# The lead-in of the first layer reordered: every modulation product and square sum on VectorE, low halves on GpSimd, low-half products last in a block

## The chip, the cores and the metric

The kernel runs on one core of one Trainium2 chip. The metric is the device time of one execution in microseconds (us), as the median of several runs. The engines are named as the profile names them: PE (TensorE; PEld is its weight load), DVE (VectorE), ACT (ScalarE), POOL (GpSimd) and SP (SyncE, which issues all transfers here). Each engine runs its own instructions in the order in which they stand; semaphores hold an instruction until its inputs are there.

## The reference

The reference is a decoder trunk of two layers with a final RMSNorm, for one sequence of 1024 positions and 1024 channels, in float32. Only the first steps of a layer matter here:

```
c_act = silu(c)                                        # once
mod = c_act @ w_ada + b_ada                            # (1, 3072): shift, scale, gate
h = rms_norm(x, norm_g) * (1.0 + scale) + shift
proj = h @ w_in
```

`proj` then feeds a causal pooling mixer, a retention mixer and an RWKV-7 mixer; their gated outputs are projected, merged, projected once more, scaled with `gate` and added to `x`. Everything of that is the same in both kernels, instruction for instruction.

## The kernel before, in words

Activations are held transposed: eight channel tiles `kt` (0 to 7) of 128 channels by 1024 positions, cut in two halves `h` (0 and 1) of 512 positions. One tile is therefore 128x512 float32, 256 KB. A float32 product is made of three faster ones: each operand is split in a rounded high part (`hhi`, `wh`, or a piece of `wbig`) and the rest (`hlo`, `wl`, or another piece of `wbig`), and PE adds high x high, low x high and high x low into one PSUM tile (`acc`), each a product of 128x128 weights with 128x512 columns.

The change touches only the **lead-in**: what comes before the first three output tiles of layer 0 (called lora, k and r, tiles 0, 1 and 2) are complete for both halves, in `acc6`. It is written out by hand under a manual schedule: for PE, DVE, ACT and POOL the order of the code is the order of the instructions. SP is not in that schedule and is ordered by the framework around it. From the end of the lead-in on, an estimated clock and lanes of tasks set the order.

The steps of the lead-in, by the names in the code:

- `xdma`, `wdma`, `aload` issue transfers on SP: the 16 tiles of `x`, the raw weights `wr` of the three output tiles (two pieces each), and 26 tiles of `w_ada` (groups 0 to 5) into a ring of eight slots (`ringG`) and six spare weight buffers (`wada`).
- `sq2(h, j)` squares two tiles on ACT and adds them on DVE (L1142), and PE sums the result over channels by four products with a column of ones (`ssps`), added up over four pairs.
- `rstd(h)` makes the reciprocal root (`rn`) on ACT and DVE, and `rstd_bc` has PE spread it over all partitions in PSUM (`rbc`); `rstd_copy` copies that to SBUF (`rbs`) for POOL.
- `normed(h, kt)` scales a tile of `x` by it, on DVE (L1176, from `rbc`) or POOL (L1174, from `rbs`).
- The modulation comes in six groups: groups 0 to 3 give shift and scale of one channel tile each (kt 0 to 3), group 4 of kt 4 and 5, group 5 of kt 6 and 7. Groups 0 and 1 are done by `ada_pe`: PE multiplies the pieces of `w_ada` as weights with a column of `cact` (16 products of 128x1 a group, `adaps<-cact,ringG`). Groups 2 to 5 are done by `ada`: DVE multiplies and adds in eight steps (L224, L226), the running sum in PSUM (`ada_ps`), the last into SBUF (`ada_acc`), and PE sums that over partitions with products of one column (`adaps<-fixed,ada_acc`). In both, `ada_end` makes `mod` (L258) and `acoef` (L264) on DVE.
- `affine(h, kt)` applies shift and scale on ACT, twice: once rounded into `hhi` (L1182), once in place (L1183). `low` subtracts them into `hlo` (L1188), on DVE or POOL.
- `wsp(j, tile)` splits a raw weight piece: a cast on ACT (L543), a subtraction on POOL (L544).
- `mms(h, kt)` issues a block: nine products, for each of the three output tiles high x high, low x high and high x low of the weights. `acc6[0]` takes half 0 and `acc6[1]` half 1.

Eight channel tiles times two halves give 16 blocks, 144 products. After them `evac` takes the six sums, and PE goes on with 48 products of the next output tile, v.

Of the kernel before, what the change touches and what calls it, by code (L numbers as in the profile page):

```python
# [96 lines left out]
def trunk_kernel(ctx, tc, xT, cvec, pos, vecs, consts, w_ada, w_all, pool_w, lora_w, out):  # L97
# [101 lines left out]
    cth = cp.tile([P, 8], F32, name="cth")  # L199
    nc.scalar.activation(cth, cact, AF.Tanh, scale=0.5)  # L200
    nc.vector.tensor_scalar(cth, cth, 0.5, 0.5, op0=ALU.mult, op1=ALU.add)
    nc.vector.tensor_tensor(cact, cact, cth, op=ALU.mult)
    nc.scalar.activation(fixed[:, 3:4], ones, AF.Sqrt)
# [7 lines left out]
    def ada(l, g, slot_, gap=2200, acc_=t_lt, ws=None):  # L211
# [23 lines left out]
        ada_end(l, g, ps)  # L235
        yield

    def ada_pe(l, g, ws):
        n = len(ADA[g][1])
        W_ = n * P  # L240
        ps = mx("adaps")
        for kt in range(NKT):
            i, o = divmod(kt * W_, HF)
            for m in range(n):
                mmul(
                    ps[:, m : m + 1], ws[i][:, o + m * P : o + (m + 1) * P], cact[:, kt : kt + 1],
                    start=(kt == 0 and m == 0), stop=(kt == NKT - 1 and m == n - 1), skip_group_check=True,
                )
            yield
# [885 lines left out]

    ssp = [None, None]

    def sq2(h, j):
# [2 lines left out]
        nc.scalar.square(b, xin[h][2 * j + 1])
        nc.vector.tensor_tensor(a, a, b, op=ALU.add)  # L1142
# [27 lines left out]
    def normed(h, *kts, pool=False):  # L1170
        for kt in kts:
            x = xin[h][kt]
            if pool:
                nc.gpsimd.tensor_tensor(x, x, rbs[h], op=ALU.mult)  # L1174
            else:
                nc.vector.tensor_tensor(x, x, rbc[h], op=ALU.mult)  # L1176
# [457 lines left out]
```

## Time and profile before

| What | Value |
| --- | --- |
| Runs | 2524.38, 2519.01, 2524.66 us; median 2524.38 |
| Profiled execution | 2522.42 us, span 2520.6 us |
| PE / DVE / ACT / POOL busy, whole span | 96% / 53% / 31% / 32% |
| Mean granted PE clock | 0.982 |
| First product of the lead-in's blocks | at 43.56 us of the span |
| The six `acoef` (shift and scale ready), starts | 37.11, 43.94, 53.93, 60.16, 67.92, 82.09 us |
| First `la` product (after the lead-in and the 48 products of v) | at 105.56 us |

The profile shows one execution. "Span" runs from the first to the last instruction; the execution's own time is 1.8 us longer. A row of the timeline reads: start, length, engine, line, operation, output<-inputs, how many, and in brackets how long the engine sat idle before it and what released it. The length of a matmul is longer than its distance to the next, since matmuls are pipelined. Rows of a grouped view read: line, engine, operation, output<-inputs, shapes, count, then busy time and the mean nanoseconds of one. Each matmul of the sums over partitions, of the modulation and of `rbc` has two records in the trace, so 32 products of the code are 64 there.

### The profile page before, as it was taken

The page shows a single profiled execution, that of the slowest core. Times are in us where ns is not written, and L with a number is a line of the kernel's source. Part 1 is how long each engine was busy: PE and PEld are TensorE (multiplying, and loading weights), DVE is VectorE, ACT ScalarE, POOL GpSimd, SP SyncE. Part 2 cuts the span into 40 slices and gives each one's busy share as a digit, 9 for nine tenths or more (in the row PEclk, how much of TensorE's full clock was granted, in tenths as well). Part 3 has the DMA queues.
Part 4 walks back from the last instruction along what each step waited for, and adds up shares of the span by engine and source line. Part 5 has one row for each costly group of instructions (what it writes and reads, how often), then busy time and mean ns, then how long its engine had stood idle before and what let it go on. Part 6 is the DMA issues. An engine that isn't in the chain of part 4 may idle for free. (4 is left out here: it accounts for less than half of the span.)

```text
span 2520.6 us, 35022 instructions
## 1 busy us (share of the span) xinstructions
PE 2425.8 (96%) x13416; PEld 2007.9 (80%) x13416; DVE 1345.5 (53%) x2548; ACT 792.1 (31%) x1465; POOL 815.7 (32%) x715
## 2 busy tenths in 40 slices
PE   7999999999999999999999999999999999999998
PEld 6778878877787787887878787788878778787888
DVE  4575467368367543467455646835745653412354
ACT  4542242332233223113444224223323312221243
POOL 2321233233133234454442232322313323236441
PEclk9999999999899999999999999999999989999999
DMA  5232112111113224676431211211211121354352
GB/s 203 80 102 72 34 43 85 34 38 60 55 54 100 83 66 134 197 224 196 146 114 50 68 38 34 77 35 43 85 43 38 60 76 51 121 156 126 105 150 76
DMA packets 124216, 223.68 MB, mean 89 GB/s; under 512 B 14096, under 2 KB 17424, under 8 KB 124048
## 3 DMA queue, kind: packets, MB, share of 16 engines
q1 hardware_dynamic: 124048, 221.44, 28.1%
q8 instruction: 105, 1.72, 0.3%
q14 instruction: 63, 0.52, 0.1%
HBM read 174.46 MB, written 46.92 MB: 88 GB/s over the span
## 5 line engine op out<-in xcount | busy, mean ns | idle before, releaser
L544 POOL TENSOR_TENSOR wl<-wr,wh 128x512 fp32r<-128x512 f32 x342 | 454.9, 1330 | 1192.8 <-ACT wh L543 1109.2
L425 PE MATMUL acc<-hhi,wh 128*128 128x512 f32 x2000 | 809.4, 405 | 16.8 <-DVE k L1011 11.0
L425 PE MATMUL acc<-hhi,wl 128*128 128x512 f32 x2000 | 810.7, 405 | 1.7 <-POOL r L1005 1.7
L425 PE MATMUL acc<-hlo,wh 128*128 128x512 f32 x2000 | 811.7, 406 | 0.0
L425 PEld LDWEIGHTS acc<-hhi,wh 128*128 128x128 f32 x2000 | 382.0, 191 | 89.7 <-DVE k L1011 12.6
L425 PEld LDWEIGHTS acc<-hhi,wl 128*128 128x128 f32 x2000 | 382.3, 191 | 71.5 <-issue 2.2
L425 PEld LDWEIGHTS acc<-hlo,wh 128*128 128x128 f32 x2000 | 382.1, 191 | 68.7 <-issue 0.7
L543 ACT CAST wh<-wr 128x512 fp32r<-128x512 f32 x342 | 211.8, 619 | 679.6 <-PE acc L425 457.5
L425 PE MATMUL acc<-olo,wh 128*128 128x512 f32 x384 | 152.9, 399 | 3.9 <-POOL olo L544 3.9
L425 PE MATMUL acc<-oG,wh 128*128 128x512 f32 x384 | 152.4, 398 | 2.2 <-ACT oG L543 1.0
L425 PE MATMUL acc<-oG,wl 128*128 128x512 f32 x384 | 151.6, 395 | 0.0
L956 DVE TENSOR_TENSOR xst<-cy,MT 64x128 f32<-64x128 f32 x128 | 36.2, 283 | 192.3 <-PE cy L425 191.8
L967 DVE SCALAR_TENSOR_TENSOR S<-ch,pc,SP 64x64 f32<-64x64 f32 x256 | 72.4, 283 | 95.0 <-PE ch L425 86.1
L889 DVE TENSOR_TENSOR tm<-MT 64x30 f32<-64x30 f32 (+14 forms) x240 | 103.4, 431 | 7.4
L953 ACT ACTIVATE SP<-S,pc 128x128 f32<-128x128 f32 x128 | 51.4, 401 | 174.0 <-DVE S L967 169.5
L895 DVE TENSOR_TENSOR MT<-MT,tm 64x30 f32<-64x30 f32 (+14 forms) x240 | 99.8, 416 | 7.5
L962 DVE COPY Z<-ch 64x128 f32<-64x128 f32 x128 | 36.1, 282 | 118.1 <-PE ch L425 117.6
L425 PEld LDWEIGHTS acc<-olo,wh 128*128 128x128 f32 x384 | 72.7, 189 | 21.6 <-POOL olo L544 5.8
L425 PEld LDWEIGHTS acc<-oG,wh 128*128 128x128 f32 x384 | 72.7, 189 | 21.1 <-ACT oG L543 2.1
L1459 DVE SCALAR_TENSOR_TENSOR gs<-gs,acc 128x512 f32<-128x512 f32 x64 | 43.4, 682 | 82.1 <-PE acc L425 70.9
L425 PEld LDWEIGHTS acc<-oG,wl 128*128 128x128 f32 x384 | 72.8, 190 | 16.6
L425 PEld LDWEIGHTS ch<-xst,G 128*128 128x128 f32 x512 | 76.7, 191 | 11.6 <-DVE xst L956 0.5
(276 smaller groups left out, 3690.4 us busy)
## 6 DMA issues: line engine op xcount, KB each, us to landing
wr<-in_w_all SPq DMA_DIRECT2D x364, 256.0 KB, 2.7
gd<-gsg SPq DMA_DIRECT2D x80, 256.0 KB, 2.0
gs<-gd SPq DMA_DIRECT2D x80, 256.0 KB, 2.9
wada<-in_w_ada SPq DMA_DIRECT2D x70, 256.0 KB, 3.1
ol<-od SPq DMA_DIRECT2D x64, 256.0 KB, 3.0
ringG<-in_w_ada SPq DMA_DIRECT2D x26, 256.0 KB, 4.3
x<-in_xT SPq DMA_DIRECT2D x16, 256.0 KB, 4.9
od<-po SPq DMA_DIRECT2D x16, 256.0 KB, 2.0
```

Of the source, the lines that this page charges most:

```text
L425: nc.tensor.matmul(out, lhsT=lhsT, rhs=rhs, start=start, stop=stop, **kw)
L543: nc.scalar.copy(hi, src)
L544: eng.tensor_tensor(lo, src, hi.bitcast(F32), op=ALU.subtract)
L889: nc.vector.tensor_tensor(pr, M3[:, i + 1 :, i : i + 1].to_broadcast([64, n, i]), M3[:, i : i + 1, 0:i].to_broadcast([64, n, i]), op=ALU.mult,
L895: nc.vector.tensor_tensor(M3[:, i + 1 :, 0:i], M3[:, i + 1 :, 0:i], pr, op=ALU.add)
L953: nc.scalar.activation(SP, S, AF.Copy, scale=pcc)
L956: nc.vector.tensor_tensor(xst[0:64, :], cy[0:64, 0:P], AV[:, c * P : (c + 1) * P], op=ALU.add)
L962: nc.vector.tensor_copy(Z[0:64, c, :], ch[0:64, 0:P])
L967: nc.vector.scalar_tensor_tensor(Sn[rw, rw], ch[rw, P + 64 * hd : P + 64 * hd + 64], pc[rw, c : c + 1], SP[rw, rw], op0=ALU.mult, op1=ALU.add,
L1459: nc.vector.scalar_tensor_tensor(s, s, 1.0, ps, op0=ALU.add, op1=ALU.mult)
```

## The change: what it does

- **Modulation.** `ada_pe` is gone; all six groups run through `ada`, eight DVE steps each. Group 0's steps stand on DVE right after the square sums; group 1's are mixed with the scaling of half 1 and two low halves.
- **Square sums.** `sq` squares one tile on ACT, and DVE adds the eight squares of a half one after the other; PE then sums once (`sums`), four products a half instead of 16.
- **Scaling.** Of the 16 tiles POOL scales eight (kt 2 to 7 of half 0, kt 4 and 5 of half 1) instead of four. DVE scales the other eight, two of them (kt 6 and 7 of half 1) from the SBUF copy `rbs`; so `rstd_copy` now runs for both halves.
- **Low halves.** POOL makes those of kt 1 to 5 (`both`), DVE those of kt 0, 6 and 7.
- **Blocks.** In `mms` the two products with `hhi` come first for each output tile, and those with `hlo` last. In the blocks of half 1 the third output tile comes after the next group's sum over partitions (`steps(gs[g], 1)`).
- **Transfers.** The raw weights of tile 2 are issued ahead of group 1's `w_ada`, not behind them. `cond_act`, which makes `cact`, moves into the manual schedule, and the table for the root is loaded once, ahead of the squares; before, three tables were loaded on ACT ahead of the first root, now two.

The lines of the diff that the prediction speaks of:

```diff
-        a, b = mo("sq"), t_lt("sq")
-        nc.scalar.square(a, xin[h][2 * j])
-        nc.scalar.square(b, xin[h][2 * j + 1])
-        nc.vector.tensor_tensor(a, a, b, op=ALU.add)
...
+    def sq(h, *kts):
+        for kt in kts:
+            t = t_lt("sq") if kt == 0 else mo("sq")
+            nc.scalar.square(t, xin[h][kt])
+            if kt == 0:
+                ssum[h] = t
+            else:
+                nc.vector.tensor_tensor(ssum[h], ssum[h], t, op=ALU.add)
...
-                mm1(acc6[h][i], wparts[i][kt // 4], kt % 4, h_cur[h][kt], kt == 0, kt == 7)
+    def mms(h, kt, *tiles):
+        r = h_cur[h][kt]
+        for b, js in ((0, (0, 1)), (1, (0,))):
+            for i in tiles or range(3):
+                for j in js:
+                    w = wparts[i][kt // 4][j][:, kt % 4 * P : kt % 4 * P + P]
+                    mmul(acc6[h][i], w, r[b], start=kt == 0 and b == 0 and j == 0, stop=kt == 7 and b == 1)
...
-        gs = [(ada_pe if g < 2 else ada)(0, g, ws=aw[g], **({} if g < 2 else dict(slot_=None))) for g in range(6)]
+        gs = [ada(0, g, None, ws=aw[g]) for g in range(6)]
...
+        def both(kt, eng=None):
+            for h in range(2):
+                affine(h, kt)
+                low(eng or G_, h, kt)
...
         wdma(0, 0)
         aload(0, 4)
-        wdma(0, 1)
+        wdma(0, 1, 2)
         aload(1, 4)
-        wdma(0, 2)
...
-        for j in range(4):
-            sq2(0, j)
+        sq(0, *range(8))
+        sums(0)
+        sq(1, 0, 1, 2)
         rstd(0)
-        sq2(1, 0)
         rstd_bc(0)
+        derive(0)
+        sq(1, 3, 4, 5, 6)
+        rstd_copy(0)
+        normed(0, 2, 3, eng=G_)
         normed(0, 0)
...
+        sq(1, 7)
+        sums(1)
+        wsp(0, 0)
+        normed(0, 4, eng=G_)
+        normed(0, 1)
+        steps(gs[0], 6)
         rstd(1)
-        wsp(0, 0)
+        steps(gs[0], 3)
+        aload(3, 2)
         rstd_bc(1)
...
+        both(2)
+        steps(gs[3], 8)
+        aload(4, 2)
         mms(0, 2)
-        steps(gs[3], 9)
...
+        mms(1, 2, 0, 1)
+        steps(gs[3], 1)
+        mms(1, 2, 2)
+        wsp(1, 1)
...
+        normed(1, 5, eng=G_)
+        both(5)
+        astep(5)
         mms(0, 4)
         mms(1, 4)
+        normed(1, 6, 7, eng=V)
         mms(0, 5)
...
+        mms(1, 5, 0, 1)
+        steps(gs[5], 1)
+        mms(1, 5, 2)
+        both(6, V)
+        both(7, V)
```

How the instructions now stand, at three places. First PE, from the second spread of the reciprocal root (`rbc`) to the first block; `acc` are the sums of the output tiles, the numbers are the tiles' own. Before:

```order
L425 MATMUL rbc_282<-cst,rn_277 128x128 x4
L425 MATMUL adaps_289<-cact,ringG_156 128x1 x16
L425 MATMUL adaps_325<-cact,ringG_156 128x1 x16
L425 MATMUL acc_373<-hhi_311,wbig_153 128x512
L425 MATMUL acc_373<-hlo_312,wbig_153 128x512
L425 MATMUL acc_373<-hhi_311,wbig_153 128x512
```

and with the change:

```order
L411 MATMUL adaps_273<-fixed,ada_acc_260 128x1 x2
L411 MATMUL rbc_280<-cst,rn_268 128x128 x4
L411 MATMUL acc_313<-hhi_293,wbig_153 128x512 x2
L411 MATMUL acc_314<-hhi_293,wbig_161 128x512 x2
L411 MATMUL acc_315<-hhi_293,wbig_164 128x512 x2
L411 MATMUL acc_313<-hlo_294,wbig_153 128x512
```

The 32 products of groups 0 and 1 have left PE, two sums over partitions have come in ahead of `rbc`, and in a block the six products with `hhi` stand ahead of the three with `hlo`.

Second, DVE from the reciprocal root to group 1's `acoef`. Before, from the root of half 1 (`rn_277`) on:

```order
L1158 RECIPROCAL rn_277<-rn_277 128x4
L258 TENSOR_TENSOR mod_99<-adaps_289,vec_91 128x2
L264 SCALAR_TENSOR_TENSOR acoef_101<-mod_99,vec_91 128x1
L1176 TENSOR_TENSOR x_137<-x_137,rbc_282 128x512
L1176 TENSOR_TENSOR x_139<-x_139,rbc_282 128x512
L1188 TENSOR_TENSOR hlo_312<-x_119,hhi_311 128x512
L1176 TENSOR_TENSOR x_141<-x_141,rbc_282 128x512
L1188 TENSOR_TENSOR hlo_320<-x_137,hhi_319 128x512
L258 TENSOR_TENSOR mod_99<-adaps_325,vec_91 128x2
L264 SCALAR_TENSOR_TENSOR acoef_101<-mod_99,vec_91 128x1
```

With the change, from the last addition of squares (`sq_211` is the sum of half 1) on:

```order
L1131 TENSOR_TENSOR sq_211<-sq_211,sq_248 128x512
L1163 TENSOR_TENSOR x_121<-x_121,rbc_222 128x512
L225 TENSOR_SCALAR ada_ps_261<-ringG_156,cact 128x256
L227 SCALAR_TENSOR_TENSOR ada_ps_261<-ringG_156,cact,ada_ps_261 128x256 x5
L1147 RECIPROCAL rn_268<-rn_268 128x4
L227 SCALAR_TENSOR_TENSOR ada_ps_261<-ringG_156,cact,ada_ps_261 128x256
L227 SCALAR_TENSOR_TENSOR ada_acc_260<-ringG_156,cact,ada_ps_261 128x256
L244 TENSOR_TENSOR mod_99<-adaps_273,vec_91 128x2
L250 SCALAR_TENSOR_TENSOR acoef_101<-mod_99,vec_91 128x1
L225 TENSOR_SCALAR ada_ps_290<-ringG_156,cact 128x256
L227 SCALAR_TENSOR_TENSOR ada_ps_290<-ringG_156,cact,ada_ps_290 128x256 x2
L1163 TENSOR_TENSOR x_137<-x_137,rbc_280 128x512
```

Group 0's eight steps now stand on DVE behind all additions; between the steps of group 1 come two scalings (the first is the last row shown) and two low halves, and two more scalings come behind them.

Third, DVE around group 5, the last. Before:

```order
L1188 TENSOR_TENSOR hlo_526<-x_127,hhi_525 128x512
L1188 TENSOR_TENSOR hlo_545<-x_129,hhi_544 128x512
L224 TENSOR_SCALAR ada_ps_582<-ringG_156,cact 128x512
L226 SCALAR_TENSOR_TENSOR ada_ps_582<-ringG_156,cact,ada_ps_582 128x512 x6
L226 SCALAR_TENSOR_TENSOR ada_acc_581<-ringG_156,cact,ada_ps_582 128x512
L258 TENSOR_TENSOR mod_99<-adaps_591,vec_91 128x4
```

and with the change:

```order
L250 SCALAR_TENSOR_TENSOR acoef_101<-mod_99,vec_91 128x2
L225 TENSOR_SCALAR ada_ps_529<-ringG_156,cact 128x512
L227 SCALAR_TENSOR_TENSOR ada_ps_529<-ringG_156,cact,ada_ps_529 128x512 x6
L227 SCALAR_TENSOR_TENSOR ada_acc_528<-ringG_156,cact,ada_ps_529 128x512
L1165 TENSOR_TENSOR x_149<-x_149,rbs_311 128x512
L1165 TENSOR_TENSOR x_151<-x_151,rbs_311 128x512
L244 TENSOR_TENSOR mod_99<-adaps_573,vec_91 128x4
```

Group 5's steps now follow group 4's `acoef` directly; the two low halves that stood ahead of them are on POOL, and two scalings stand behind them.

More of the change, by code (lines that the diff above doesn't have):

```diff
@@ L197, in vv, with cond_act @@
         return vec[l][:, o : o + 1]
[L199 to L203, printed above, removed]
+    def cond_act():
+        cth = cp.tile([P, 8], F32, name="cth")
+        nc.scalar.activation(cth, cact, AF.Tanh, scale=0.5)
+        nc.vector.tensor_scalar(cth, cth, 0.5, 0.5, op0=ALU.mult, op1=ALU.add)
+        nc.vector.tensor_tensor(cact, cact, cth, op=ALU.mult)
+        nc.scalar.activation(fixed[:, 3:4], ones, AF.Sqrt)
     def ada_load(l, g, slot_, ws, n):
@@ L234, in ada @@
             mmul(ps[:, m : m + 1], acc[:, m * P : (m + 1) * P], ones)
[L235 to L249, printed above, removed]
         ada_end(l, g, ps)
@@ L1217, in trunk_kernel, with astep @@
         aw = [[] for _ in range(6)]
-        gs = [(ada_pe if g < 2 else ada)(0, g, ws=aw[g], **({} if g < 2 else dict(slot_=None))) for g in range(6)]
+        gs = [ada(0, g, None, ws=aw[g]) for g in range(6)]
         def aload(g, n):
             ada_load(0, g, wada_slot, aw[g], n)
+        def both(kt, eng=None):
+            for h in range(2):
+                affine(h, kt)
+                low(eng or G_, h, kt)
+        def astep(g, nxt=None):
+            for _ in range(8):
+                steps(gs[g], 1)
+                if nxt is not None:
+                    aload(nxt, 1)
+        cond_act()
         xdma(0, *range(8))
@@ L1246, in trunk_kernel @@
[L1246 to L1250 removed]
+        steps(gs[0], 6)
         rstd(1)
[L1252 removed]
+        steps(gs[0], 3)
+        aload(3, 2)
         rstd_bc(1)
[L1254 to L1256 removed]
+        wsp(0, 1, 2)
+        steps(gs[1], 2)
+        affine(0, 0)
+        steps(gs[1], 1)
         normed(1, 0)
[L1258 removed]
+        low(V, 0, 0)
+        affine(1, 0)
@@ L1259, in trunk_kernel @@
+        steps(gs[1], 2)
         normed(1, 1)
-        low(V, 0, 0)
-        wsp(0, 1)
-        affine(1, 0)
-        normed(1, 2)
         low(V, 1, 0)
-        steps(gs[1], 9)
+        steps(gs[1], 3)
+        rstd_copy(1)
+        acc6[0] = [acc_ps() for _ in range(3)]
+        mms(0, 0)
+        normed(1, 2, 3)
+        acc6[1] = [ps_c.tile([P, HF], F32, tag=t, name=nm("acc"), bufs=n) for t, n in (("ch", 1), ("cy", 2), ("cy", 2))]
+        mms(1, 0, 0, 1)
+        steps(gs[1], 1)
+        mms(1, 0, 2)
@@ L1266, in trunk_kernel @@
+        normed(0, 5, 6, eng=G_)
+        both(1)
         wdma(1, 0, 1, 2)
         aload(4, 6)
-        affine(0, 1)
-        normed(1, 3)
-        wsp(0, 2)
-        low(V, 0, 1)
-        affine(1, 1)
-        normed(1, 4, 5, 6, 7)
-        low(G_, 1, 1)
-        acc6[0] = [acc_ps() for _ in range(3)]
-        mms(0, 0, 1)
-        acc6[1] = [ps_c.tile([P, HF], F32, tag=t, name=nm("acc"), bufs=n) for t, n in (("ch", 1), ("cy", 2), ("cy", 2))]
-        mms(1, 0)
-        steps(gs[2], 9)
-        affine(0, 2)
@@ L1294, in trunk_kernel @@
+        steps(gs[3], 1)
+        mms(1, 2, 2)
+        wsp(1, 1)
+        both(3)
+        wsp(1, 2)
+        normed(1, 4, eng=G_)
+        astep(4, 5)
         mms(0, 3)
-        wsp(1, 1, 2)
-        for _ in range(8):
-            steps(gs[4], 1)
-            aload(5, 1)
+        mms(1, 3, 0, 1)
         steps(gs[4], 1)
-        affine(0, 4)
-        low(V, 0, 4)
-        affine(1, 4)
-        low(G_, 1, 4)
-        mms(1, 3)
-        affine(0, 5)
-        low(V, 0, 5)
-        affine(1, 5)
```

69 lines of the change are left out of this document (20 added, 49 removed).

## The prediction

> **What bounds the kernel now.** I read the page first, then busy time by stretches, then the engines' timelines of the first 106 us.
>
> ```profile
> PE 2425.8 (96%) x13416; PEld 2007.9 (80%) x13416; DVE 1345.5 (53%) x2548; ACT 792.1 (31%) x1465; POOL 815.7 (32%) x715
> x<-in_xT SPq DMA_DIRECT2D x16, 256.0 KB, 4.9
> 0.00:30.05 30.05, 18.27 (x80) 17.63 (x81) 10.62 (x23) 15.07 (x25) 4.83 (x13) 1.00 0.83 298
> 30.05:43.56 13.51, 13.51 (x65) 13.51 (x65) 3.50 (x7) 3.67 (x5) 3.52 (x5) 1.00 0.27 78
> 43.56:82.09 38.53, 31.29 (x125) 23.13 (x126) 27.90 (x53) 17.71 (x24) 14.02 (x11) 0.97 0.42 138
> 82.09:94.36 12.27, 12.27 (x46) 9.84 (x45) 3.90 (x7) 11.85 (x19) 5.38 (x7) 0.81 0.17 43
> ```
>
> PE bounds the whole, so what moves the end is a stretch in which PE does no products of blocks. Those stand at the start: 30.05 us until the second spread of the root ends, 13.5 us of modulation on PE (busy 13.51 of 13.51, while DVE works 3.5), and 38.5 us in which PE is busy only 31.3. (Columns: stretch and length, then busy of PE, PEld, DVE, ACT, POOL.) The lead-in is the whole subject, since behind it nothing changes. The timelines say what each wait is for:
>
> ```profile
> 30.05 13.65 PE L425 MATMUL adaps<-cact,ringG 128*128 128x1 f32 x64
> 80.02 1.84 PE L425 MATMUL adaps<-fixed,ada_acc 128*128 128x1 f32 x8 [3.06 <-DVE ada_acc L226]
> 36.91 0.16 DVE L258 TENSOR_TENSOR mod<-adaps,vec 128x2 f32<-128x2 f32 x1 [8.79 <-PE adaps L425]
> 37.11 0.16 DVE L264 SCALAR_TENSOR_TENSOR acoef<-mod,vec 128x1 f32<-128x1 f32 x1
> 43.94 0.16 DVE L264 SCALAR_TENSOR_TENSOR acoef<-mod,vec 128x1 f32<-128x1 f32 x1
> 53.93 0.16 DVE L264 SCALAR_TENSOR_TENSOR acoef<-mod,vec 128x1 f32<-128x1 f32 x1
> 60.16 0.16 DVE L264 SCALAR_TENSOR_TENSOR acoef<-mod,vec 128x1 f32<-128x1 f32 x1
> 67.92 0.16 DVE L264 SCALAR_TENSOR_TENSOR acoef<-mod,vec 128x2 f32<-128x2 f32 x1
> 73.59 0.75 DVE L224 TENSOR_SCALAR ada_ps<-ringG,cact 128x512 f32<-128x512 f32 x1
> 82.09 0.16 DVE L264 SCALAR_TENSOR_TENSOR acoef<-mod,vec 128x2 f32<-128x2 f32 x1
> 105.56 0.49 PE L425 MATMUL la<-lt,lw 64*128 64x512 f32 x1
> ```
>
> The six `acoef` are the pace: no block of a channel tile can start before its own. DVE waits 8.79 us for PE's modulation, then PE waits for DVE's, and group 5 starts on DVE 5.5 us after group 4 is through, behind low halves that wait for ACT. The mark at which the lead-in has been paid is the first `la` product at 105.56, and from 82.09 to there PE hardly stops.
>
> **The change part by part.** I walk DVE's new order through with these lengths:
>
> ```profile
> 5.93 5.36 SPq L1133 DMA_DIRECT2D x<-in_xT  x8
> 14.18 0.62 ACT L1141 ACTIVATE sq<-x 128x512 f32<-128x512 f32 x1
> 24.51 0.68 DVE L1142 TENSOR_TENSOR sq<-sq,sq 128x512 f32<-128x512 f32 x1
> 49.34 3.11 DVE L226 SCALAR_TENSOR_TENSOR ada_ps<-wada,cact,ada_ps 128x256 f32<-128x256 f32 x6
> 61.02 4.71 DVE L226 SCALAR_TENSOR_TENSOR ada_ps<-ringG,cact,ada_ps 128x512 f32<-128x512 f32 x6
> 46.43 2.48 DVE L1176 TENSOR_TENSOR x<-x,rbc 128x512 f32<-128x512 f32 x4
> 37.30 0.81 ACT L1182 ACTIVATE hhi<-x,mod,acoef 128x512 fp32r<-128x512 f32 x1 [8.88 <-DVE acoef L264]
> 38.15 0.81 ACT L1183 ACTIVATE x<-x,mod,acoef 128x512 f32<-128x512 f32 x1
> L1188 POOL TENSOR_TENSOR hlo<-x,hhi 128x512 fp32r<-128x512 f32 x8 | 10.3, 1291 | 26.8 <-ACT x L1183 26.8
> 53.12 0.58 PE L425 MATMUL adaps<-fixed,ada_acc 128*128 128x1 f32 x4 [0.17 <-DVE ada_acc L226]
> 66.66 1.02 PE L425 MATMUL adaps<-fixed,ada_acc 128*128 128x1 f32 x8 [1.14 <-DVE ada_acc L226]
> ```
>
> A modulation step takes 0.52 us (3.11/6) at 256 columns and 0.79 (4.71/6) at 512, a scaling 0.61 (2.48/4), an addition 0.7, a pair on ACT 1.6, a low half on POOL 1.28, the sums 0.45 and 0.9.
>
> - *Square sums.* The last tile of `x` is issued at 10.9 (the last of eight from 5.93 to 11.29) and lands 4.9 us later, at 15.8 to 16.3. Its square (0.62), a scaling ahead of the addition (0.61), the addition (0.7), another scaling (0.61) and some 0.5 for starting beside POOL (below): group 0's first step at 19.3. The other additions fit earlier: 0.72 each, behind ACT's squares. PE loses 24 of 32 one-column products here; it idles anyway.
> - *Group 0*: 8 x 0.52 + 0.1 for a reciprocal = 4.25, its sums at the slow pace of the early rows (0.85), `mod` and `acoef` 0.35: `acoef` at 24.8, for 37.1 before. Its transfers are issued behind `x` as before and through by then.
> - *Group 1*: eight steps 4.16, four scalings and two low halves 3.7, waits 0.4: 33.1, for 43.94.
> - *Groups 2 and 3*: here the steps (4.2) are no longer the longest way. PE's sums now stand behind two products with a low half from POOL, so the way is two pairs on ACT 3.2, POOL 1.28, two products 0.45, sums 0.45, `mod` and `acoef` 0.35, semaphores 0.3: 6.05 each, `acoef` at 39.1 and 45.2. Before, group 3 took 6.23 (53.93 to 60.16).
> - *Group 4*: 8 x 0.79 + 0.9 + 0.45 = 7.7, as before (60.16 to 67.92 is 7.76): 52.9.
> - *Group 5*: its steps end at 59.3, but its sums stand behind the low half of kt 5, half 1, whose scaling is POOL's. POOL makes the low halves of kt 4 (54.8 to 57.6, behind ACT), then that scaling (to 58.9); ACT's pair takes 1.7, POOL's low half 1.3, two products and the sums 1.35, `mod` and `acoef` 0.35: 63.6, for 82.09. So 10.7 us against 14.2, and POOL, not DVE, is what is late next.
> - *Behind the last `acoef`*: 85 products to `la`, three of which are of the block before. The lengths:
>
> ```profile
> 82.72 1.05 PE L425 MATMUL acc<-hhi,wbig 128*128 128x512 f32 x2
> 86.56 0.68 PE L425 MATMUL acc<-hhi,wbig 128*128 128x512 f32 x2
> 93.45 0.61 PE L425 MATMUL acc<-hhi,wbig 128*128 128x512 f32 x2
> 95.49 0.61 PE L425 MATMUL acc<-hhi,wbig 128*128 128x512 f32 x2
> ```
>
> Nine products take 3.84 us from 82.72 to 86.56, 0.43 each, but 2.04 from 93.45 to 95.49, 0.227 each. The slow pace lasted from 80.02 to 86.5, behind the wait of 3.06. In the new order no wait of PE inside the blocks is over 1.4 us, so I take 0.227: 85 x 0.227 = 19.3 plus 2.6 of waits for ACT's last pairs = 21.9, for 23.5 before (105.56 - 82.09).
>
> `la` then comes at 63.6 + 21.9 = 85.5, and **the sum is 105.56 - 85.5 = 20.1 us**, of which 12.3 are there at the first `acoef`, 18.5 at the last, and 1.6 come behind it. The blocks themselves, 144 products, are the same in another order, which by itself is worth nothing: PE does the `hhi` products while POOL is busy, and its waits of 0.5 to 0.8 us per block go to where POOL's low half is late. One table load less on ACT (1.28) lies ahead of the squares and in the old wait for the sums; nothing.
>
> *The queues.* On SP the weights of the fourth item stand among the last loads of group 4 and wait for POOL's splits. By the walk the eighth load then lands near 48.4 and is used near 51.0; each us that POOL is later than 2.6 would cost one. Group 1's loads:
>
> ```profile
> 10.00:20.00 10.00, 7.24 (x32) 6.86 (x32) 2.17 (x5) 4.07 (x7) 0.00 (x0) 1.00 1.05 385
> ```
>
> The tile of weights now issued ahead of them is 256 KB at 385 GB/s, 0.7 us; they land at 21.5 to 23.5, ahead of the first step that needs them at 24.9. Without that cover it would cost the 0.7.
>
> *Unknown costs.* POOL beside DVE:
>
> ```profile
> 94.81 1.29 POOL L544 TENSOR_TENSOR wl<-wr,wh 128x512 fp32r<-128x512 f32 x1 [1.46 <-ACT wh L543]
> 95.39 1.27 DVE L544 TENSOR_TENSOR lw<-lraw,lw 128x512 fp32r<-128x512 f32 x1 [1.89 <-ACT lw L543]
> 55.87 1.27 POOL L1188 TENSOR_TENSOR hlo<-x,hhi 128x512 fp32r<-128x512 f32 x1 [6.63 <-ACT x L1183]
> 56.09 1.54 DVE L226 SCALAR_TENSOR_TENSOR ada_ps<-ringG,cact,ada_ps 128x256 f32<-128x256 f32 x3
> ```
>
> A DVE subtraction with two SBUF inputs took 1.27 instead of 0.69: it ended only 0.6 behind POOL's. Modulation steps, with one input in PSUM, ran beside POOL at their 0.52. Additions and low halves on DVE are of the first kind: one addition and two low halves of the new order may meet POOL, 0 to 3 x 0.6, so 0 to +1.8; I take 0.5, since the other additions come before POOL's first scaling. The landing of `x`: 4.9 at the median, 5.4 for its neighbours, +-0.5. Below, nothing can start group 0 before 18.3, so 1 us earlier at most. The rest of the program in its own pace: the three runs lie 5.6 us apart, +-2.8.
>
> [...]
>
> **The rivals.** *The clock is withheld.* PE's products are slow at first:
>
> ```profile
> L425 PE MATMUL acc<-hhi,wbig 128*128 128x512 f32 x7 | 4.4, 696 | 0.1
> ```
>
> (between 43.5 and 49 us, against 390 later), although 13.65 us of modulation had kept PE busy. In my walk the first block has the slow pace, from 26.4 to 31.6, hidden under group 1. If the pace stayed slow through all blocks, because each has two waits and sums of one column, the way from one `acoef` to the next would be 0.85 to the first high part, 15 products 6.4, sums 0.85 and 0.35, so 8.4 instead of 6.05 for groups 2 and 3, and 4 more for groups 4, 5 and the end together: +8.7 us, a time of 2511. For it: around group 4's `acoef` a stretch of 3.5 us holds three products only. Against it: 66.66 shows a wait of 1.14 and sums of 1.02 in one stretch and no slowing, and only 3.06 of waiting brought it. [...] The trace shows one drop, with 0.81 granted from 82.09 to 94.36.
>
> *The gain is given back.* If a chain behind the lead-in had a fixed time, PE would wait for it: the time within 0.3%. The order of all engines behind the lead-in is the same, and its transfers hang on the same instructions, so nothing there has a time of its own; against it also that ACT takes up the sums some 2.5 us ahead of v's first product, and `la`, the first product that needs them, comes 11 us later still. About 2520.
>
> *POOL becomes the bound, and the kernel is slower.* Place: kt 1 to 5, where POOL has two low halves, a split or a scaling each, up to four operations a pair. It decides from 6.05/4 = 1.5 us for one. To eat all, five pairs of four must last 20.1 us longer: 2.5 us for one; at 2.9 the time is 2522.4 - 20.1 + 5 x (11.6 - 6.05) = 2530.
>
> ```profile
> L544 POOL TENSOR_TENSOR wl<-wr,wh x342: 1262/1292/1883, 91.8 to 2495.7; 128x512 fp32r<-128x512 f32 x171
> ```
>
> The longest of 342 such operations took 1.88, at the median 1.29. So hardly.
>
> **How the numbers follow.** The sum is made against the profiled execution of 2522.4 (span 2520.6 and 1.8 around it): 2502.3. The median shown is 2524.4, the lowest run 2519.0; I predict 2503. The likeliest case has 0.87, the withheld clock 0.08, the gain given back 0.03, POOL 0.02. What a measurement can tell from no change is 0.3%, 7.6 us: faster 0.95 (the first two), same 0.03, slower 0.02. Low end: 1 us of earlier start and 2.8 of the runs' spread, with 1.5 for waits of the walk taken too long, 2497. High end: 1.8 - 0.5 of contention, 0.5 of landing, 2.8 of spread give 2507; to take in most of the withheld clock I go to 2511.
>
> **What would show it.** `la` near 85.5, the six `acoef` near 24.8, 33, 39, 45, 53 and 63.6, and no more than 1.4 us of PE waiting at once between the first block and `la`. Additions of squares that last 1.2 us show contention; block products that lie 0.43 apart behind 32 us show the clock; POOL operations above 1.5 us, or a step of group 4 idle for a DMA, the queues. It is wrong if group 0's steps start after 21, or if `la` gains 20 and the span does not.

## The result, and the profile after

| | before | changed |
| --- | --- | --- |
| Median, us | 2523.95 (4 runs, 2519.01 to 2524.66) | 2501.99 (4 runs, 2500.36 to 2504.22) |
| Profiled execution, us | 2522.42, span 2520.6 | 2501.75, span 2499.9 |
| First `la` product | 105.56 | 88.65 |
| From `la` to the end | 2415.04 | 2411.25 |

The ratio of the means is 0.9918, 95% interval 0.9901 to 0.9935: faster by 0.8%. (All ratios here are of runs in the fast state; one run of dve_mod_only, 3180.33 us at a granted clock of 0.698, is left out for that.) The sum of the prediction was 2502.3 us for the profiled execution, and it took 2501.75. That agreement is better than the steps behind it: the lead-in gained 16.9 us, not 20.1, and 3.8 us came from behind `la`, where both kernels run the same instructions.

Busy time of the changed kernel, from its page and from the view of busy time by stretches (columns: stretch and length, busy of PE, PEld, DVE, ACT, POOL, granted clock, DMA share, GB/s), cut at the first, second and sixth `acoef`, at the first product of v and at `la`:

```profile
PE 2397.6 (96%) x13312; PEld 1980.1 (79%) x13312; DVE 1357.1 (54%) x2564; ACT 791.9 (32%) x1465; POOL 822.8 (33%) x721
0.00:25.46 25.46, 7.02 (x30) 6.58 (x31) 16.08 (x36) 15.22 (x26) 9.03 (x16) 1.00 0.95 336
25.46:34.20 8.74, 6.90 (x27) 5.06 (x26) 8.52 (x16) 3.85 (x5) 2.57 (x4) 1.00 0.97 345
34.20:66.81 32.61, 28.77 (x116) 21.27 (x117) 25.03 (x46) 17.29 (x23) 20.91 (x17) 0.90 0.34 115
66.81:77.45 10.64, 9.58 (x39) 6.78 (x38) 4.53 (x8) 10.29 (x17) 3.53 (x3) 1.00 0.09 24
```

PE's 13.5 us of modulation are gone, and blocks are multiplied from 27.6 on. DVE is full in group 1's stretch (8.52 of 8.74) and POOL uses 2.57 there: the work there is one-sided. The granted clock between the second and the sixth `acoef` is 0.90; from 43.56 to 82.09 us of before it was 0.97. The rows that answer to those shown of before, from the timelines, with POOL's scalings that begin beside the first `acoef`:

```profile
19.96 0.47 DVE L225 TENSOR_SCALAR ada_ps<-ringG,cact 128x256 f32<-128x256 f32 x1
25.43 2.49 POOL L1165 TENSOR_TENSOR x<-x,rbs 128x512 f32<-128x512 f32 x2
25.46 1.24 DVE L250 SCALAR_TENSOR_TENSOR acoef<-mod,vec 128x1 f32<-128x1 f32 x1
34.20 0.16 DVE L250 SCALAR_TENSOR_TENSOR acoef<-mod,vec 128x1 f32<-128x1 f32 x1
41.18 0.29 DVE L250 SCALAR_TENSOR_TENSOR acoef<-mod,vec 128x1 f32<-128x1 f32 x1
47.60 0.16 DVE L250 SCALAR_TENSOR_TENSOR acoef<-mod,vec 128x1 f32<-128x1 f32 x1
55.36 0.16 DVE L250 SCALAR_TENSOR_TENSOR acoef<-mod,vec 128x2 f32<-128x2 f32 x1
66.81 0.16 DVE L250 SCALAR_TENSOR_TENSOR acoef<-mod,vec 128x2 f32<-128x2 f32 x1
88.65 0.49 PE L411 MATMUL la<-lt,lw 64*128 64x512 f32 x1
```

The first `acoef`, one element per partition, lasts 1.24 us where all of them took 0.16 before: as long as the first of POOL's two scalings, 2.49 us together, which began 0.03 us ahead of it. From the sixth `acoef` to `la` it is 21.84 us.

**Where the other 3.8 us came from.** Setting the two traces side by side, product by product from `la` on, one place stands out: over a stretch of small and large products late in the program, before takes 10.3 us more than the changed kernel. The view by stretches there, first before, then changed:

```profile
2064.00:2088.00 24.00, 24.00 (x158) 18.26 (x158) 0.28 (x1) 5.17 (x9) 1.28 (x1) 0.52 0.06 23
```

```profile
2052.00:2066.20 14.20, 14.20 (x159) 11.01 (x158) 0.28 (x1) 5.07 (x9) 1.09 (x1) 1.00 0.10 38
```

The same 158 weight loads, PE busy throughout in both, at half the clock in one (0.52) and at full clock in the other. Smaller drops elsewhere, some in one trace and some in the other, take 6.5 us of that back. So the rest is a matter of when the clock falls, and the experiments had to tell whether the change has a part in it.

### The profile page after: what moved, and what is told of

Its sections match the earlier page's. It is cut to its first block, busy times and chain, and to the rows that moved or that the text cites. A ratio compares the mean times of both kernels' runs of the same rounds, so it can differ in the third digit from the quotient of the medians.

```text
span 2499.9 us, 34854 instructions
## 1 busy us (share of the span) xinstructions
PE 2397.6 (96%) x13312; PEld 1980.1 (79%) x13312; DVE 1357.1 (54%) x2564; ACT 791.9 (32%) x1465; POOL 822.8 (33%) x721
## 5 line engine op out<-in xcount | busy, mean ns | idle before, releaser
L411 PEld LDWEIGHTS ch<-xst,G 128*128 128x128 f32 x512 | 76.7, 191 | 11.6 <-DVE xst L942 0.5
```

The source lines that it names most:

```text
L411: nc.tensor.matmul(out, lhsT=lhsT, rhs=rhs, start=start, stop=stop, **kw)
```

## The experiments

Each is told by its first `la` product. Since the landing of `x` moves the start from run to run (the last square of the new order began between 16.46 and 17.78 us), it is also told by the time from group 0's first modulation step to `la` (68.69 us in the changed kernel). Where an edit moves the first step itself, the time from the last square says more (71.57 us in the changed kernel).

| Run | Last square | First step | `acoef`, those that matter | `la` | Step to `la` | `la` to end |
| --- | --- | --- | --- | --- | --- | --- |
| before | | | 37.11, 43.94 ... 82.09 | 105.56 | | 2415.04 |
| before_again | | | 37.13, 43.95 ... 81.29 | 104.05 | | 2405.15 |
| changed | 17.08 | 19.96 | 25.46, 34.20, 41.18 ... 66.81 | 88.65 | 68.69 | 2411.25 |
| after_again | 16.77 | 19.64 | 25.14, 33.89, 40.82 ... 66.54 | 88.39 | 68.75 | 2411.1 |
| dve_mod_only | | 27.68 | 33.16, 43.24 ... 80.36 | 103.10 | | 2414.7 |
| pe_mod | 17.55 | | 28.93, 37.47 ... 73.19 | 95.05 | | 2407.3 |
| tile_order | 17.53 | 20.45 | 25.96, 35.81 ... 77.11 | 100.10 | 79.65 | 2429.1 |
| old_loads | 17.33 | 20.20 | 25.70, 33.72 ... 66.32 | 88.17 | 67.97 | 2417.5 |
| psum_sq | 17.78 | 20.19 | 25.69, 34.09 ... 66.90 | 88.72 | 68.53 | 2411.9 |
| fill | 16.46 | 19.34 | 24.85, 33.58, 39.80, 47.00 ... 66.17 | 88.03 | 68.69 | 2416.1 |
| acoef_ps | 16.81 | 21.00 | 26.30, 34.18, 40.29, 46.51 ... 65.64 | 87.75 | 66.75 | 2417.8 |
| fill_acoef_ps | 17.10 | 21.29 | 26.60, 34.48, 40.62, 46.85 ... 65.96 | 88.06 | 66.77 | 2410.5 |
| sums5_late67 | 17.20 | 20.09 | 25.59, 34.32 ... 55.47, 64.90 | 86.76 | 66.67 | 2418.8 |
| combined | 16.62 | 19.24 | 24.55, 30.94, 36.79, 42.62, 50.27, 60.53 | 82.62 | 63.38 | 2420.9 |

### Both kernels again: whose are the 3.8 us?

No edit.

> The changed kernel once more, unaltered. Theory A (the lead-in's gain is 16.9 us, and the other 3.8 us of the profiled pair lie in the rest of the program only because PE's clock happened to fall at other moments): la is again at 88.65 +- 1.5, and the stretch from la to the end, 2411.25 us in the first profile of it and 2415.04 in that of the kernel before, comes out anywhere from 2408 to 2418, with the half-clock stretches at other places than before. Theory B (the change itself makes the rest 3.8 us shorter): la to the end is 2411.2 +- 0.5 again.

> The kernel before once more. Over the ten traces so far the time from la to the end, for the same instructions, lies between 2407.3 and 2429.1 us, and the stretches of half clock in it add up to 76 to 122 us. Theory 'the rest is the clock's own': la at 105.5 +- 1.0, and la to the end again anywhere from 2407 to 2429, near 2373 plus 0.47 times the half-clock time. Theory 'the kernel before has a slower rest than the changed one': 2415 +- 1 as in its first trace.

The rest of the program, from `la` to the end, in the views by stretches of before (first trace, then the second) and of the changed kernel:

```profile
105.56:2520.60 2415.04, 2339.29 (x13056) 1934.77 (x13055) 1293.31 (x2448) 737.66 (x1381) 784.61 (x676) 0.98 0.28 86
```

```profile
104.05:2509.20 2405.15, 2329.17 (x13056) 1928.18 (x13055) 1292.28 (x2448) 737.03 (x1381) 783.02 (x676) 0.99 0.27 86
```

```profile
88.65:2499.90 2411.25, 2334.12 (x13056) 1931.42 (x13055) 1297.02 (x2448) 737.69 (x1381) 782.84 (x676) 0.98 0.28 86
```

The same 13056 products each time. after_again alone fitted both theories (88.39, and 2411.1 to the end); in its second trace the kernel before has the shorter rest by 6 us, which only theory A allows. So the 3.8 us do not belong to the change. Over all 14 traces the rest runs from 2405 to 2429 us, and a straight line through the half-clock time recorded in it (67 to 122 us) gives 2376 us plus 0.43 us for each us of half clock, with what is left over at 1.1 us.

The times say the same in their way. In this comparison the changed kernel's median was 2508.58 us (8 runs, 2501.23 to 2517.28) against 2520.17 (23 runs, 2508.64 to 2527.07): ratio 0.9949, interval 0.9929 to 0.9970, 11.6 us of the medians against 22.0 in the first. (The kernel before had medians of 2524, 2520 and 2514 us in the three larger comparisons, the last two of them on different chips, so times are set side by side only within one comparison.) The lead-in's gain, 105.56 or 104.05 less 88.65 or 88.39, is 15.4 to 17.2 us, between the two.

### What the parts are worth

dve_mod_only, the kernel before with one line changed:

```diff
-        gs = [(ada_pe if g < 2 else ada)(0, g, ws=aw[g], **({} if g < 2 else dict(slot_=None))) for g in range(6)]
+        gs = [ada(0, g, None, ws=aw[g]) for g in range(6)]
```

> The kernel before with one edit: groups 0 and 1 of the modulation on VectorE too, every other instruction at its old place in the code. Theory 'PE's 13.5 us of modulation are the gain': la comes some 12 us earlier, near 93, and the time falls by 12. Theory 'the new order carries the gain': group 0's eight steps start only behind VectorE's old work (about 28.1), so its acoef is near 33.4 instead of 37.11; group 1's steps stand behind three scalings, a low half and waits for ScalarE, acoef near 43.3 instead of 43.94; then all goes on at the old pace: la near 104.6, 1 us earlier than 105.56, time within 0.1% of before apart from the runs' spread.

`la` at 103.10: 1 to 2.5 us, and in time nothing (ratio 1.0016, interval 1.0000 to 1.0033). DVE, from its timeline:

```profile
33.16 0.16 DVE L264 SCALAR_TENSOR_TENSOR acoef<-mod,vec 128x1 f32<-128x1 f32 x1
33.23 1.28 DVE L1176 TENSOR_TENSOR x<-x,rbc 128x512 f32<-128x512 f32 x2
35.05 0.69 DVE L1188 TENSOR_TENSOR hlo<-x,hhi 128x512 fp32r<-128x512 f32 x1 [0.54 <-ACT x L1183]
37.73 0.48 DVE L224 TENSOR_SCALAR ada_ps<-ringG,cact 128x256 f32<-128x256 f32 x1
43.24 0.16 DVE L264 SCALAR_TENSOR_TENSOR acoef<-mod,vec 128x1 f32<-128x1 f32 x1
```

The first `acoef` gains 4 us and the second 0.7: group 1's steps stand behind scalings and low halves that wait for ACT. Taking 13.65 us of work off PE gives almost nothing by itself.

pe_mod is the changed kernel with that one line as before (and `ada_pe` back).

> The changed kernel with one part undone: groups 0 and 1 of the modulation on PE again (32 products of one column, 13.65 us in the kernel before), all else in the new order. Theory 'moving the modulation is the whole gain of the lead-in': la back near 105 (88.65 + 16.9). Theory 'the gain has two halves, and the other one is that the work starts earlier and in another order': PE begins group 0 near 20 as soon as the weights land, so the first acoef is near 28, the second, behind 6.8 us more of PE, near 37, and la near 96.5, 8 us behind the changed kernel and 9 ahead of the kernel before.

`la` at 95.05, 6.4 us behind the changed kernel (5.9 from the last square on) and 9.0 to 10.5 ahead of before: the second theory. PE does group 0 from 21.74 (6.96 us) and group 1 from 30.41 (6.83), so the new order brings the larger part of the gain even with the modulation on PE.

tile_order:

```diff
-        for b, js in ((0, (0, 1)), (1, (0,))):
-            for i in tiles or range(3):
-                for j in js:
+        for i in tiles or range(3):
+            for b, j in ((0, 0), (1, 0), (0, 1)):
...
```

> The changed kernel with one edit: in a block the products of one output tile stand together again (high x high, then the low half of the activation, then the low half of the weights), so a block's second product needs hlo. The prediction's step ('by itself worth nothing, the waits only move'): la within 0.5 us of the changed kernel's 88.65. The rival: PE now stands at the second of nine products until POOL's low half is there, 1.3 us behind ScalarE's second pass, with eight products still to do behind it; for groups 2, 3 and 5 that lies on the way to the next acoef: about 1 us more for each of groups 2 and 3, 1.5 for 4 and 5 together and the rest at the start, la near 93.5, time 5 us longer than the changed kernel, and more waits of PE for POOL's hlo.

`la` at 100.10, 11.5 us behind the changed kernel (11.0 from the first step on), over twice the rival's price; time ratio to before 0.9985, interval 0.9959 to 1.0010. Who PE waited for from 24 to 100 us (total, times, longest), and the stretches:

```profile
PE acc L411 <- POOL hlo L1177: 6.8, 4, 1.7
47.60:51.00 3.40, 3.40 (x10) 2.60 (x9) 1.34 (x4) 0.00 (x0) 1.60 (x2) 0.50 0.44 139
54.40:61.20 6.80, 5.77 (x14) 4.51 (x15) 3.89 (x6) 1.67 (x3) 4.73 (x4) 0.50 0.86 271
64.70:71.50 6.80, 5.55 (x13) 4.39 (x14) 6.22 (x8) 4.53 (x6) 5.98 (x5) 0.50 0.00 0
```

In the changed kernel the waits for POOL's `hlo` are 1.1 us in all. Here PE stands 1.7 us at the second product of four blocks, and three stretches, 17 us together, run at half clock. How the 11 us divide between the waits and the clock, no run shows. The order of products within a block, taken as nothing in the prediction, is worth that much once POOL makes the low halves.

old_loads:

```diff
-        wdma(0, 1, 2)
+        wdma(0, 1)
         aload(1, 4)
+        wdma(0, 2)
```

> The changed kernel with the third output tile's raw weights issued behind group 1's weights of the modulation again, as before. The prediction: worth nothing, 0.7 us at most without the cover: la 88.5 +- 0.7. Rival, 'the new order of transfers feeds the first block': with the old one the third tile's split on ScalarE and POOL comes some 2.5 us later (four transfers of 256 KB at 385 GB/s), POOL's scalings behind it too, and the second acoef with la by about 0.5.

`la` at 88.17, 0.7 us earlier from the first step on: within the bound, and not the rival's way. Its first `acoef` took 0.16 us, with POOL's scaling beginning 0.1 us behind it and not ahead of it:

```profile
25.70 0.16 DVE L250 SCALAR_TENSOR_TENSOR acoef<-mod,vec 128x1 f32<-128x1 f32 x1
25.80 2.51 POOL L1165 TENSOR_TENSOR x<-x,rbs 128x512 f32<-128x512 f32 x2
```

The second `acoef` came 13.52 us behind the first step instead of 14.24, and that is the 0.7 at `la`. Which of the two begins first is a matter of 0.1 us, and it leads to the next question.

### Why the lead-in gained 3 us less than the sum

Two causes were open: the two half-clock stretches, and DVE standing beside POOL.

fill, with seven products that nobody reads:

```diff
         ps = mx("adaps")
+        for _ in range(FILL.get((l, g), 0)):
+            mmul(ps, wparts[0][0][0][:, 0:P], h_cur[0][0][0])
...
+    FILL = {(0, 1): 4, (0, 4): 3}
```

> The changed kernel with seven added products that nobody reads: four 128x512 products ahead of group 1's sums over partitions and three ahead of group 4's, into the bank that the sums then overwrite; PE waits 0.80 and 0.79 us at these places. Theory 'PE's clock is withheld': both half-clock stretches (36 to 39 and 56 to 60 us) follow a stretch of 3.4 us in which PE did only four and five products; with the added ones it does eight, so the granted clock stays 1.00 from 30 us on, the products of blocks lie 0.23 apart throughout, the third acoef comes near 40.3 instead of 41.18, the sixth near 65 instead of 66.81, la near 86.5 instead of 88.65. Theory 'the shortfall is contention of VectorE with POOL': the clock stays up, but la moves by less than 0.5 us, since the added products fill waits only. If the clock falls all the same, neither.

The stretches of 3.41 us around the drops, in the changed kernel and in fill:

```profile
32.39:35.80 3.41, 2.05 (x9) 1.49 (x10) 3.28 (x8) 1.37 (x2) 0.00 (x0) 1.00 0.61 176
35.80:39.21 3.41, 3.41 (x9) 2.43 (x8) 2.45 (x6) 2.29 (x4) 2.81 (x3) 0.50 0.00 0
52.87:56.28 3.41, 2.26 (x13) 1.38 (x12) 2.10 (x6) 0.66 (x1) 2.05 (x2) 1.00 1.00 339
56.28:59.69 3.41, 3.20 (x8) 2.55 (x9) 3.27 (x5) 3.31 (x6) 2.07 (x2) 0.50 0.41 153
```

```profile
32.39:35.80 3.41, 2.64 (x13) 1.93 (x13) 3.23 (x9) 1.99 (x3) 0.27 (x1) 1.00 0.56 160
35.80:39.21 3.41, 2.84 (x15) 2.00 (x13) 1.90 (x4) 1.68 (x3) 3.14 (x3) 1.00 0.00 0
52.87:56.28 3.41, 2.83 (x16) 1.87 (x15) 2.20 (x5) 1.28 (x2) 1.46 (x2) 1.00 0.93 309
56.28:59.69 3.41, 2.83 (x13) 2.03 (x12) 3.23 (x6) 3.34 (x5) 2.71 (x3) 1.00 0.24 93
```

The clock stayed up, and from the first step to `la` it is 68.69 us, as before the edit. So the first theory falls: the drops are real, and taking them away alone gains nothing. (That the seven products held the clock is likely, not shown, since in acoef_ps, sums5_late67 and old_loads it stayed up without them: 1.00 from 30.8 us to `la` in sums5_late67, and in the other two six `hhi` products behind 34 us took 1.67 at most, against 2.93 from 56.49 in the changed kernel.) Why nothing came of it stands in fill's DVE and POOL rows:

```profile
39.80 1.07 DVE L254 SCALAR_TENSOR_TENSOR acoef<-mod,vec 128x1 f32<-128x1 f32 x1
39.57 1.28 POOL L1169 TENSOR_TENSOR x<-x,rbs 128x512 f32<-128x512 f32 x1
62.60 1.77 POOL L1181 TENSOR_TENSOR hlo<-x,hhi 128x512 fp32r<-128x512 f32 x1 [0.53 <-ACT x L1176]
```

The third `acoef` came 0.8 us earlier from the first step on and then stood beside nearly the whole of POOL's scaling, of which it had met only the end in the changed kernel (0.29); in group 5 PE's faster products waited for POOL's last low half. So the drop of group 2 and the shut-out of the third `acoef` hide each other, and this run does not say what the drop would cost without the shut-out.

acoef_ps makes `acoef` from the sums in PSUM, with the 1 added to `b_ada` at the start:

```diff
+        if l == 0 and g < 6:
...
+                nc.vector.scalar_tensor_tensor(
+                    acoef[0][:, c + i : c + i + 1], ps[:, i : i + 1], vec[0][:, o + i : o + i + 1],
+                    vec[0][:, a + i : a + i + 1], op0=ALU.add, op1=ALU.mult,
+                )
...
+        for s_ in (slice(o, o + 8, 2), slice(o + 8, o + 10), slice(o + 12, o + 14)):
+            nc.vector.tensor_scalar_add(vec[0][:, s_], vec[0][:, s_], 1.0)
```

> The changed kernel with one edit: acoef is made by VectorE straight from the sums in PSUM, (sum + b + 1) times norm_g, with the 1 added to b at the start, so that it no longer reads two inputs from SBUF. Theory 'VectorE is shut out by POOL': the first acoef, which began at 25.46 in the changed kernel and lasted 1.24 us beside a scaling on POOL, lasts under 0.2; the first hhi comes at 25.6 instead of 26.74, the first step of group 1 at 25.6 instead of 26.63 and the second acoef near 33.1 instead of 34.20; la near 87.6 instead of 88.65. Theory 'the length of 1.24 us is a wait that the record shows at the wrong place' (for the sums, say): the first hhi stays at 26.7 and la at 88.65 +- 0.4. If only the clock matters behind group 1, the second acoef moves and la does not.

```profile
26.30 0.22 DVE L247 SCALAR_TENSOR_TENSOR acoef<-adaps,vec 128x1 f32<-128x1 f32 x1 [1.17 <-PE adaps L420]
40.29 0.22 DVE L247 SCALAR_TENSOR_TENSOR acoef<-adaps,vec 128x1 f32<-128x1 f32 x1 [1.77 <-PE adaps L420]
```

`la` is at 87.75, 66.75 us from the first step, 1.9 less than in the changed kernel. Of these, 1.1 are there at the second `acoef` (13.18 us behind the first step instead of 14.24): the first theory, and the shut-out by itself. The other 0.9 come in group 2, where the changed kernel had the dropped clock and fill the shut-out; this run had neither, so they are the share of both together.

The first step stands at 21.00 although the last square came earlier here than in the changed kernel (16.81 for 17.08): 4.19 us lie between the two instead of 2.88. The three small additions to `b_ada` move the additions of squares back by 0.2 us, and the fourth of them, which had begun 0.2 us ahead of POOL's first scaling, now meets it and lasts 1.8 us (the second of these two):

```profile
16.21 2.60 DVE L1140 TENSOR_TENSOR sq<-sq,sq 128x512 f32<-128x512 f32 x2
16.99 2.94 POOL L1174 TENSOR_TENSOR x<-x,rbs 128x512 f32<-128x512 f32 x2 [0.73 <-ACT rbs L1166]
```

In the changed kernel the same two additions, from 16.28 on, took 1.49. So the edit gives back 1.3 us at the start, and from the last square to `la` it gains 0.6. The second edit on top of it:

> Both edits: the seven added products, which kept PE's clock up, and acoef from PSUM. With the added products alone the third acoef came 1.0 us earlier and then lasted 1.07 us beside POOL's scaling, the fourth came only 0.3 earlier, la at 88.03. Theory 'clock and shut-out each hide the other': together they carry, third acoef near 38.8, fourth near 45.1, la near 86.3 (2.3 earlier than the changed kernel). Theory 'something else sets groups 3 to 5' (POOL's low halves, PE's own work): the third acoef comes near 38.8, but la within 0.6 of the 88.03 of the added products alone.

66.77 us from the first step, and the same late first step: the seven products add nothing to `acoef` from PSUM either, the second theory at `la`. It is a weak test, since the clock was up in acoef_ps already.

psum_sq keeps the running sum of squares in PSUM:

```diff
-            t = t_lt("sq") if kt == 0 else mo("sq")
+            t = acc_ps() if kt == 0 else mo("sq")
...
+                o = t_lt("sq") if kt == 7 else ssum[h]
+                nc.vector.tensor_tensor(o, ssum[h], t, op=ALU.add)
```

> The changed kernel with the running sum of squares in PSUM, so that VectorE's additions have one input in SBUF. In the changed kernel the last addition took 1.16 us and POOL's first two scalings 3.30 together (1.28 each where nothing stands beside them), and group 0's first step came at 19.96 (19.3 predicted). Theory 'VectorE and POOL shut each other out there': the last addition takes 0.7, POOL's pair 2.5, the first step comes 0.4 to 0.6 earlier against the last tile of x, and la with it by at most that. Theory 'the start hangs on the landing of x alone': the addition is shorter and the first step stays where it is, counted from the last square.

The start of the changed kernel, then of psum_sq:

```profile
17.08 0.63 ACT L1127 ACTIVATE sq<-x 128x512 f32<-128x512 f32 x1
17.26 3.30 POOL L1165 TENSOR_TENSOR x<-x,rbs 128x512 f32<-128x512 f32 x2 [0.93 <-ACT rbs L1157]
18.28 1.16 DVE L1131 TENSOR_TENSOR sq<-sq,sq 128x512 f32<-128x512 f32 x1
```

```profile
17.78 0.63 ACT L1127 ACTIVATE sq<-x 128x512 f32<-128x512 f32 x1
17.96 2.51 POOL L1167 TENSOR_TENSOR x<-x,rbs 128x512 f32<-128x512 f32 x2 [0.92 <-ACT rbs L1159]
18.99 0.69 DVE L1132 TENSOR_TENSOR sq<-acc,sq 128x512 f32<-128x512 f32 x1
```

From the last square to the first step 2.41 us instead of 2.88, both sides free: the 0.5 of the prediction for this place, and `x` landed 0.7 later in this run, which hides it in `la`.

sums5_late67:

```diff
-        normed(1, 6, 7, eng=V)
         mms(0, 5)
-        mms(1, 5, 0, 1)
         steps(gs[5], 1)
-        mms(1, 5, 2)
+        mms(1, 5)
+        normed(1, 6, 7, eng=V)
```

> The changed kernel with two moves around group 5: its sums over partitions go ahead of the block of kt 5, half 1, not behind two thirds of it, and VectorE's two scalings from SBUF go behind the acoef of group 5. In the changed kernel VectorE is through with group 5's steps at 61.73 and waits 2.75 us for the sums, which PE does at 65.63; POOL's last low half takes 1.77 us beside the two scalings. Theory 'the sums stand too late': the sixth acoef comes near 64.6 instead of 66.81, PE's waits of 0.48 and 0.58 behind it shrink, la near 87.3. Theory 'PE is full there anyway': the sixth acoef moves by 2 us and la by less than 0.4, since PE's products are only put in another order.

Changed kernel, then this run:

```profile
61.64 2.22 DVE L1165 TENSOR_TENSOR x<-x,rbs 128x512 f32<-128x512 f32 x2
63.24 1.77 POOL L1177 TENSOR_TENSOR hlo<-x,hhi 128x512 fp32r<-128x512 f32 x1 [0.53 <-ACT x L1172]
66.61 0.16 DVE L244 TENSOR_TENSOR mod<-adaps,vec 128x4 f32<-128x4 f32 x1 [2.75 <-PE adaps L411]
```

```profile
64.90 0.16 DVE L250 SCALAR_TENSOR_TENSOR acoef<-mod,vec 128x2 f32<-128x2 f32 x1
64.98 1.29 DVE L1165 TENSOR_TENSOR x<-x,rbs 128x512 f32<-128x512 f32 x2
```

`la` at 86.76, 2.0 us less from the first step on: the sums stood too late, and the two scalings, 2.22 us beside POOL, take 1.29 by themselves. The clock stayed up in this run, but that is not the cause: from the fifth to the sixth `acoef` fill, with the clock up too, took 11.47 us and the changed kernel 11.45, this run 9.43. The run does not separate the two moves.

### What the runs point to, in one kernel

combined is the changed kernel with acoef_ps, psum_sq and sums5_late67, with more work moved from DVE to POOL in group 1, and with the sums of groups 1 to 3 earlier (the lines of group 1):

```diff
         normed(1, 0)
         low(V, 0, 0)
+        rstd_copy(1)
         affine(1, 0)
         steps(gs[1], 2)
-        normed(1, 1)
-        low(V, 1, 0)
+        normed(1, 1, eng=G_)
+        low(G_, 1, 0)
         steps(gs[1], 3)
...
-        normed(1, 2, 3)
+        normed(1, 2, 3, eng=G_)
...
-        mms(1, 0, 0, 1)
         steps(gs[1], 1)
-        mms(1, 0, 2)
+        mms(1, 0)
```

> What the runs point to, in one kernel built on the changed one: acoef from PSUM, the running sum of squares in PSUM, group 5's sums ahead of kt 5, half 1, the sums of groups 1 to 3 earlier too (ahead of kt 0, half 1, and behind the first output tile of kt 1 and 2), the scalings of kt 1 to 3 of half 1 and the low half of kt 0, half 1, on POOL, which stood idle from 27.9 to 36.1 us, with the copy of the root for it on ScalarE earlier. Theory: the edits carry 1.0 (acoef), 1.9 (group 5), 0.5 (start) and about 1.5 (group 1 free of VectorE's four operations), la near 84 with PE's clock up, 4.5 us earlier than the changed kernel; in time 4.5 us less than the changed kernel on this chip (2508.6), so 2504, with the rest anywhere in its spread. Rival: one of the limits that hid the others takes over (POOL's queue in group 2, or a drop of the clock), and la stays above 86.5.

```profile
30.94 0.22 DVE L247 SCALAR_TENSOR_TENSOR acoef<-adaps,vec 128x1 f32<-128x1 f32 x1 [0.70 <-PE adaps L420]
82.62 0.49 PE L420 MATMUL la<-lt,lw 64*128 64x512 f32 x1
82.62:2503.50 2420.88, 2345.20 (x13056) 1938.78 (x13055) 1292.58 (x2448) 737.34 (x1381) 782.22 (x676) 0.98 0.27 85
```

`la` at 82.62, 6 us ahead of the changed kernel (5.3 from the first step on), more than expected. The time does not show it: median 2503.09 of 12 runs (2492.38 to 2518.06) against 2514.00 for before (17 runs in the same comparison), ratio 0.9950, interval 0.9930 to 0.9971, close to the changed kernel's second ratio; the profiled execution had the second longest rest of all. The lead-in beats both kernels, and the time that of before; that the time beats the changed kernel's is open.

## Why the prediction was right, point by point

`la` came 3.15 us later than the sum had it (88.65 for 85.5). In the sum's own terms that is 0.66 at group 0's start, 0.44 in group 1, 0.93 in group 2, 0.37 in group 3, 0.75 in group 5, and nothing elsewhere.

- **Group 0's start, 19.3.** 19.96 and 19.64. The 0.5 for DVE beside POOL was there (0.47). The rest is the landing of `x`: the walk has it by 16.3, and the last square began at 17.08, 16.46 to 17.78 over the runs, a little more than the +-0.5 allowed.
- **The first two `acoef`, 24.8 and 33.1.** 25.46 and 34.20. Here is the step that failed: "additions and low halves on DVE are of the first kind: one addition and two low halves of the new order may meet POOL". The 128x1 `acoef` has two SBUF inputs too, and it waited for a whole scaling on POOL, 1.08 us; DVE's next step and ACT's first pair waited with it. Group 1 lost only 0.44 against the sum, since the rest of its walk was too long (7.88 us without the shut-out, in acoef_ps, for 8.3). The total for contention was taken as 0.5, with 1.8 as the bound. Measured on the way to `la` were 0.47 for the addition, 1.08 for `acoef` and 0.49 for POOL's last low half (below): 2.0.
- **Groups 2 and 3, 6.05 each.** 6.98 and 6.42 in the changed kernel, where the first is the dropped clock; 6.20 and 7.19 in sums5_late67, where the second is `acoef` beside POOL; 6.11 and 6.22 in acoef_ps, without either. The mechanism was right. The 0.37 of group 3 in the changed kernel have no run of their own.
- **Group 4, 7.7.** 7.76.
- **Group 5, 10.7, "POOL, not DVE, is what is late next".** 11.45. POOL's last low half ended at 65.01 and the sums followed; it took 1.77, held up by DVE's two scalings, which the sum had not counted as meeting POOL; with the scalings behind it, it took 1.27 in sums5_late67 and 1.30 in combined. The prediction reckoned with contention on DVE's side alone. The rows show it on POOL's side too (1.77 for 1.27 or 1.30, and 3.30 for its first two scalings, which took 2.51 in psum_sq, where the addition read PSUM).
- **Behind the last `acoef`, 21.9.** 21.84, with two small errors against each other: the trace has 87 products there, not 85, which is 0.45 us more at 0.227 each, and as much less of waits.
- **The order of products, "by itself worth nothing".** Wrong by 11 us as a price of the part, and without effect on the sum, since the walk had the new order in it.
- **No wait over 1.4 us and full pace.** The longest wait between the blocks was 0.80, yet the clock fell twice (0.50 from 35.80 and from 56.28): the withheld clock came in part. Taking it away alone gained nothing at `la`; what it cost beside the shut-out, and what in tile_order, is open.
- **The loads, nothing.** 0.7 us against the change, by way of POOL's start; inside the bound given.
- **POOL as the bound.** No: its low halves lasted 1.34 on the mean, the longest 1.77.
- **The span.** That the sum came out to 0.6 us is luck: the lead-in gained 3.2 us less than the sum, and the rest happened to be 3.8 us shorter in this pair. In the second comparison the medians lay 11.6 us apart, about half of what was forecast. The prediction's +-2.8 for the rest was too small: 24 us lie between the shortest and the longest of 14 traces.

## What to carry to other kernels

Count every instruction that reads two SBUF operands beside a busy POOL, a one-column one too: the first `acoef` lasted 1.24 us beside the first of POOL's two scalings (2.49 together), 0.16 where POOL began 0.1 us behind it (old_loads), and 0.22 with its sums read from PSUM while POOL's two scalings ran from 24.15 to 26.65 (combined, at 24.55). When work is moved off the bounding engine, price the order of everything around it, for the move alone may give nothing and the order most. And judge an edit of a few us at the start by a landmark behind it, not by the span, when the rest of the program varies by more, counted from a point that the edit itself does not move: from the first step acoef_ps gained 1.9 us, from the last square 0.6.
